# Twelve feed-forward tiles in eight products in place of seven, with the input sums four tiles later

## The chip, the cores and the metric

The kernel runs on one core of a Trainium2 chip. A core has a matrix engine (TensorE, PE in the profile, with its weight loads shown apart as PEld), three engines for elementwise work (VectorE or DVE, ScalarE or ACT, GpSimd or POOL), and a queue that issues transfers from the chip's memory (SyncE, SP). They run beside one another and wait for each other by semaphores. The metric is the device time of one execution in microseconds (us). The kernel before was timed in three runs with a median of 2261.39 us.

## What is computed

The reference is the trunk of an encoder on one sequence of 512 tokens with 1024 features, in float32. It has two layers of the form feed-forward, token mixer, feed-forward, so there are six sublayers, which the kernel numbers 0 to 5. Sublayers 0, 2, 3 and 5 are feed-forward, sublayer 1 is a state-space mixer and sublayer 4 is differential attention. Each sublayer takes its input scaled and shifted by vectors that a projection of the condition `c` gives, adds its result, gated, to the residual stream and normalizes:

```python
def swiglu(u, w_gate, w_up, w_down):
    return (jax.nn.silu(u @ w_gate) * (u @ w_up)) @ w_down
...
        mods = (cond @ ada_w[i] + ada_b[i]).reshape(b, N_SUB, 3, D_MODEL)
        gate = lambda s: (1 + mods[:, s, 2])[:, None, :]
        y = swiglu(modulate(x, mods[:, 0]), ffn_w_gate[i, 0], ffn_w_up[i, 0], ffn_w_down[i, 0])
        x = layer_norm(ALPHA * x + 0.5 * gate(0) * y, ln_g[i, 0], ln_b[i, 0])
...
        y = swiglu(modulate(x, mods[:, 2]), ffn_w_gate[i, 1], ffn_w_up[i, 1], ffn_w_down[i, 1])
        x = layer_norm(ALPHA * x + 0.5 * gate(2) * y, ln_g[i, 2], ln_b[i, 2])
```

The hidden size of the feed-forward sublayers is 2816, which is 22 tiles of 128 features.

## The kernel before

**Layout.** Features lie on the 128 partitions and the 512 tokens along the free dimension. An input `u` is eight tiles of 128 x 512. Each float32 operand is split into a rounded high part and a low part (`uh` and `ul`, `wh` and `wl`), and a product of two of them is three matmuls: high by high, high by low, low by high (`mm3`, L162). A split of a weight tile of 128 x 1024 is a copy on ACT (L119) and a subtraction on DVE (L120).

**A feed-forward layer** (`ffn`) goes through its 22 tiles in three parts of 8, 7 and 7 (`FPARTS`). In each part it makes the hidden tiles from the gate and up weights; then eight down products (`down_units`), one for each tile of the output, sum over the part's hidden tiles and are added to the residual stream by DVE (L366, `add_res`). In the last part the down products also feed the normalization, which ends the layer and makes the next layer's `uh` and `ul` (L348 to L350). When that is done, POOL scales the residual stream (L359, L360, `residual`), while the next layer's first tiles are under way.

**A hidden tile can be made in two ways.**

- Direct: two products over eight input tiles, one for gate and one for up. That is 48 matmuls of 512 columns (in tiles 0 to 2 of layers 2, 3 and 5 they are 96 of 256 columns, since the halves of the tokens are taken one after the other). SiLU on ACT (L533), a multiplication on DVE (L535) and a split of the result follow.
- In seven products (`seven`): gate and up together are regarded as a product of two-by-two blocks, which takes seven block products in place of eight, each over four pairs of input tiles. That is 84 matmuls of 256 columns. The block products need sums of the weights, made for each tile (`weight_forms`: four sums in place, L459; four splits, L449 on ACT and L450 on DVE), and sums of the inputs, made once for each layer (`input_forms`: for each of four pairs of input tiles two additions, four sums of halves and two splits, L426 to L432). DVE and ACT put the products together (L482 to L498).

**Where each is used.** The parameter `first7` of `ffn` is the first tile that is made in seven products; in layer 0 it is 22, so there all tiles are direct. The input sums are made one pair at a time at the four tiles ahead of `first7`, right after each tile's hidden result is split. In layer 0 these are tiles 18 to 21. There the sums are made as well, though nothing uses them.

**The stream.** The 72 modulation vectors of each of the two layers of the reference are made by DVE from weight tiles of 512 KB, one unit each (`ada_unit`, L180). A generator hands them out: `advance(stream, per[0])` draws `per[0]` units after each direct tile, and `advance(stream, per[1])` draws `per[1]` after each down product of the first two parts. Layers 2 and 3 draw one after a direct tile and two after a down product. A tile in seven products draws none.

**Order and buffers.** Loads go through SP's queue in program order into four buffers of 128 x 1024 (`raw`), which the stream shares. The engines' instructions are laid out by a scheduler at build time, so work of neighbouring tiles is interleaved on each engine; at run time each engine takes its list in that order. Split weights go into rings of three buffers in each of two pools (`ring`). Hidden tiles and input sums share 32 buffers (`big`).

The lines that matter for the change are these: `ffn` decides by `if f >= first7` which way a tile is made, and makes the input sums under `if first7 - 4 <= f < first7`; the calls stand at the end of `hybrid_trunk`.

Of the kernel before, what the change touches and what calls it, by code (L numbers as in the profile page):

```python
# [46 lines left out]
def hybrid_trunk(tc, xT, cb, par, cst, adaw, wgu, wdn0, wdn1, wdn2, wdt, win, wso, wqk, wv, wao, dist_in, dtp, lam_in, out):  # L47
# [17 lines left out]
    def tmp(name="tmp"):  # L65
        return tp.tile([P, T], F32, tag="t", name=name)

    def acc(tag="acc"):
        return ps.tile([P, T], F32, tag=tag, name=tag, bufs=BANKS[tag])
# [21 lines left out]
    def load(src, n=1024):  # L91
        raw = wp.tile([P, 1024], F32, tag="raw", name="raw", bufs=4)
        nc.sync.dma_start(raw[:, :n], src)
        return raw[:, :n]
# [7 lines left out]
    def split(raw, where=None):  # L102

        n = raw.shape[-1]
        if where == "a":
            hi, lo = [], []
            for o in range(0, n, T):
                r = raw[:, o : o + T]
                h, l = big(F32R, "wah"), big(F32R, "wal")
                x = nc.scalar.activation(h, r, AF.Copy)  # L110
                eng = nc.vector if first_split[0] or o else nc.gpsimd
                y = eng.tensor_tensor(out=l, in0=r, in1=h.bitcast(F32), op=ALU.subtract)  # L112
                for a, b in zip((x, y), behind):
                    tc.add_manual_dep(a.ins, b.ins.name, NOSYNC, reason="inputs before weights")
                hi.append(h)
                lo.append(l)
            return [(hi[c // T][:, c % T : c % T + P], lo[c // T][:, c % T : c % T + P]) for c in range(0, n, P)]
        hi, lo = ring()
        nc.scalar.activation(hi[:, :n], raw, AF.Copy)  # L119
        nc.vector.tensor_tensor(out=lo[:, :n], in0=raw, in1=hi[:, :n].bitcast(F32), op=ALU.subtract)  # L120
        return Unit(hi, lo, n)
# [20 lines left out]
    def split_act(src, scale=None):  # L142
        hi, lo = big(F32R, "hi"), big(F32R, "lo")
        split_into(hi, lo, src, scale)
        return hi, lo
# [22 lines left out]
    def proj(o, w, u, m=P, cols=FULL, prev=None):  # L168
        for a, b in cols:
            prev = mm3(  # L170
                o[:m, a:b], [(w[k][0], w[k][1], u[k][0][:, a:b], u[k][1][:, a:b]) for k in range(len(u))], prev
            )
        return prev
# [47 lines left out]
    def ada_stream(l, js):  # L221
        for j in js:
            ada_unit(l, j)
            if (j + 1) % 8 == 0:
                s, ty = divmod(j // 8, 3)
                n = l * 3 + s
                if ty == 1 and n > 0:
                    make_shift_scale(n)
                elif ty == 2:
                    make_gate(n)  # L230
            yield

    def advance(g, n):
        for _ in range(n):
            if g is None or next(g, "end") == "end":
                return
# [136 lines left out]
    def first_units(n):  # L373

        if n == 1:
            src = [win[e] for e in range(2)]
        elif n == 4:
            src = [wqk[0, e] for e in range(2)]
        else:
            src = [wgu[{2: 1, 3: 2, 5: 3}[n], j // 2, j % 2] for j in range(3)]  # L380
        return [split(load(x), "a") for x in src]
# [39 lines left out]
    def input_forms(u):  # L421

        for k in range(4):
            top, bot = tmp("ft"), tmp("fb")
            for o, d in ((top, k), (bot, k + 4)):
                nc.vector.tensor_tensor(out=o, in0=u[d][0].bitcast(F32), in1=u[d][1].bitcast(F32), op=ALU.add)  # L426
            t5, t7, t4, t2 = top[:, :H], top[:, H:], bot[:, :H], bot[:, H:]
            nc.vector.tensor_tensor(out=t5, in0=t5, in1=t7, op=ALU.subtract)
            nc.vector.tensor_tensor(out=t7, in0=t7, in1=t2, op=ALU.subtract)
            nc.vector.tensor_tensor(out=t2, in0=t2, in1=t5, op=ALU.add)  # L430
            nc.vector.tensor_tensor(out=t4, in0=t4, in1=t2, op=ALU.subtract)
            (th, tl), (bh, bl) = split_act(top), split_act(bot)  # L432

            def half(x, j):
                return tuple(y[:, j * H : (j + 1) * H] for y in x)

            yield {
                1: half(u[k], 0), 2: half(u[k + 4], 0), 3: half(u[k + 4], 1),
                5: half((th, tl), 0), 7: half((th, tl), 1), 4: half((bh, bl), 0), 6: half((bh, bl), 1),
            }  # L440
# [30 lines left out]
    def seven(raw_g, raw_u, forms, hs):  # L471

        w = weight_forms(raw_g, raw_u)

        def product(j, o, **kw):
            return mm3(o, [(*w[j][k], *forms[k][j]) for k in range(4)], **kw)

        A, B, C = acc(), acc(), acc("mid")
        px, sg, up = tmp("px"), tmp("sg"), tmp("up")
        y, x = px[:, :H], px[:, H:]  # L480
        product(1, A[:, :H])
        nc.scalar.activation(y, A[:, :H], AF.Copy)  # L482
        product(6, B[:, :H])
        nc.vector.tensor_tensor(out=x, in0=y, in1=B[:, :H], op=ALU.subtract)
        yield
        product(5, C[:, :H])
        last = product(2, A[:, :H], start=False)
        nc.scalar.activation(sg[:, :H], A[:, :H], AF.Silu)
        product(7, B[:, :H], start=False)
        nc.vector.tensor_tensor(out=y, in0=B[:, :H], in1=y, op=ALU.subtract)  # L490
        nc.vector.tensor_tensor(out=up[:, H:], in0=y, in1=C[:, :H], op=ALU.subtract)  # L491
        product(4, A[:, H:], after=last)
        nc.vector.tensor_tensor(out=up[:, :H], in0=y, in1=A[:, H:], op=ALU.add)
        yield
        product(3, C[:, :H], start=False)
        nc.vector.tensor_tensor(out=x, in0=x, in1=C[:, :H], op=ALU.add)
        nc.scalar.activation(sg[:, H:], x, AF.Silu)
        nc.vector.tensor_tensor(out=sg, in0=sg, in1=up, op=ALU.mult)  # L498
        hs.append(split_act(sg))


    def ffn(n, stream=None, per=(0, 0), pre=None, first7=FT):


        forms, making = [], None
        sc = ExitStack()
        extra[0] = sc.enter_context(tc.tile_pool(name=f"wx{n}", bufs=3))
        idx = {0: 0, 2: 1, 3: 2, 5: 3}[n]
        u = next_u[0]
        f = 0  # L510
        pre = pre or first_units(n)
        for pi, nf in enumerate(FPARTS):
            hs = []
            open7 = None
            for _ in range(nf):
                if f >= first7:
                    g = seven(load(wgu[idx, f, 0]), load(wgu[idx, f, 1]), forms, hs)
                    next(g)
                    if open7 is not None:
                        next(open7, None)  # L520
                    next(g)
                    open7 = g
                    f += 1
                    continue
                wg, wu = (pre.pop(0) if pre else split(load(wgu[idx, f, e])) for e in range(2))
                cols = HALVES if f < 3 and n > 0 else FULL
                tag = "mid" if f == 2 else "ln" if f == 3 and n == 0 else "acc"
                pg = acc(tag)
                proj(pg, wg, u, cols=cols)
                pu = acc(tag)  # L530
                proj(pu, wu, u, cols=cols)
                sg = tmp("sg")
                nc.scalar.activation(sg, pg, AF.Silu)  # L533
                h = tmp("h")
                nc.vector.tensor_tensor(out=h, in0=sg, in1=pu, op=ALU.mult)  # L535
                hs.append(split_act(h))
                if first7 - 4 <= f < first7:
                    making = making or input_forms(u)
                    forms.append(next(making))
                f += 1  # L540
                if f > 3 or n > 0:
                    advance(stream, per[0])

            if open7 is not None:
                next(open7, None)

            def mk(d):
                return lambda: [(d, split(load(wdn[pi][idx, d], nf * P)))]

            for _ in down_units(n, hs, [mk(d) for d in range(KT)], pi == len(FPARTS) - 1):  # L550
                if pi < 2:
                    advance(stream, per[1])
        extra[0] = None
        sc.close()
# [497 lines left out]
    advance(st0, 100)  # L1052
    ssm(1)
    st1 = ada_stream(1, range(72))
    ffn(2, st1, (1, 2), first7=4)
    ffn(3, st1, (1, 2), first7=4)
    advance(st1, 100)
    attention(4)
    ffn(5, first7=4)
    ctx.close()  # L1060


# [99 lines left out]
```

## Time and profile before

| | |
|---|---|
| median of three runs | 2261.39 us (2259.89 to 2261.66) |
| the profiled execution | 2260.94 us |
| its span, first to last instruction | 2259.2 us |
| granted TensorE clock, mean | 0.988 |
| PE busy | 2170.5 us, 96% |
| DVE busy | 1746.3 us, 77% |
| ACT busy | 989.0 us, 44% |
| POOL busy | 403.5 us, 18% |
| read from memory | 289.53 MB |

A page of the profile gives the busy time of each engine, a chain of work followed back from the last instruction, and groups of instructions by line. In a row such as `L162 PE MATMUL acc<-hi,wh 128*128 128x512 f32`, L162 is the line of the kernel, `acc` is what is written, `hi` and `wh` are what is read. A number in square brackets at the end of a row of the timeline is the time for which the engine stood idle before that instruction, with the instruction that released it. Matmuls are pipelined and their ends are modelled: the time from one to the next is what they cost. A view of stretches gives for each the busy time and count of instructions of each engine, the granted clock of TensorE (PEclk, 1.00 is full speed), the share of the transfer engines' time and the rate in GB/s. All times are counted from the start of the span.

The feed-forward layers 2, 3 and 5 begin their first product at 834.6, 1216.4 and 1880.1 us.

### The profile page before, as it was taken

The numbers are of one execution on the slowest core, as the hardware profiler recorded it, in microseconds if no ns is written. First come the engines' busy times: TensorE is split into PE (matmuls) and PEld (weight loads), VectorE is DVE, ScalarE is ACT, GpSimd is POOL, SyncE is SP. The second block draws the span as 40 slices with busy tenths as digits, with TensorE's granted clock in tenths as the row PEclk, the third lists the DMA queues.
The fourth block names the chain that finished last, engine by engine and source line by source line (L and its number), as shares of the span: only waits on it lengthen the run. The fifth ranks groups of instructions, "written<-read, shape, count | busy, mean of one in ns | idle before, by whom it ended". The sixth has DMA issues, their size and how long they took to land.

```text
span 2259.2 us, 33641 instructions
## 1 busy us (share of the span) xinstructions
PE 2170.5 (96%) x13030; PEld 1866.5 (83%) x13030; DVE 1746.3 (77%) x2850; ACT 989.0 (44%) x1648; POOL 403.5 (18%) x412
## 2 busy tenths in 40 slices
PE   7999999999999988999999899999999999899998
PEld 5788889866777677898999889899877779889897
DVE  6864668656766689998888998897866679959696
ACT  4422234567656534343453334343555544425353
POOL 3000003344222335000014200003300025100003
PEclk9999999999999999999999999999999999999999
DMA  8864652564544413646442273633211111323231
GB/s 301 281 212 161 206 169 78 124 174 141 163 125 128 126 47 112 215 140 201 145 131 76 83 252 102 234 110 115 67 57 57 57 60 63 102 86 106 91 114 46
DMA packets 88545, 296.97 MB, mean 131 GB/s; under 512 B 9536, under 2 KB 12992, under 8 KB 88384
## 3 DMA queue, kind: packets, MB, share of 16 engines
q1 hardware_dynamic: 88384, 294.81, 40.9%
q8 instruction: 102, 1.67, 0.3%
q14 instruction: 59, 0.48, 0.1%
HBM read 289.53 MB, written 5.24 MB: 130 GB/s over the span
## 4 chain that ended last, share of the span: by engine, by line
PE 54%; DVE 17%; issue 5%; ACT 3%; DMA 2%; POOL 2%; POOLq 0%; ACTq 0%; DVEq 0%; SPq 0%
PE acc L162 42%; PE mid L162 5%; DVE wl L120 2%; DVE raw L459 2%; PE mid L782 2%; DVE lo L150 1%; DVE wl L450 1%; DMA raw<-in_wdn 1%; DVE ul L350 1%; DVE raw L180 1%; PE mid L931 1%; PE ln L162 1%; DVE lt L348 1%; ACT wh L119 1%; PE ln L249 1%
## 5 line engine op out<-in xcount | busy, mean ns | idle before, releaser
L162 PE MATMUL acc<-hi,wh 128*128 128x512 f32 (+1 forms) x1488 | 506.6, 341 | 20.0 <-ACT wh L449 10.0
L162 PE MATMUL acc<-hi,wl 128*128 128x512 f32 (+1 forms) x1488 | 505.9, 340 | 5.5 <-DVE wl L450 5.5
L162 PE MATMUL acc<-lo,wh 128*128 128x512 f32 (+1 forms) x1488 | 504.9, 340 | 0.0
L162 PE MATMUL acc<-uh,wh 128*128 128x512 f32 (+1 forms) x1256 | 442.6, 353 | 4.5 <-ACT px L482 4.4
L162 PE MATMUL acc<-ul,wh 128*128 128x512 f32 (+1 forms) x1256 | 439.7, 350 | 0.1
L162 PE MATMUL acc<-uh,wl 128*128 128x512 f32 (+1 forms) x1256 | 438.5, 350 | 1.3 <-DVE wl L120 1.3
L119 ACT ACTIVATE wh<-raw 128x1024 fp32r<-128x1024 f32 (+1 forms) x234 | 239.2, 1027 | 410.1 <-PE acc L162 212.1
L120 DVE TENSOR_TENSOR wl<-raw,wh 128x1024 fp32r<-128x1024 f32 (+1 forms) x234 | 288.0, 1232 | 86.5 <-ACT wh L119 77.5
L162 PEld LDWEIGHTS acc<-hi,wh 128*128 128x128 f32 x1488 | 283.5, 191 | 58.0 <-ACT wh L449 10.6
L162 PEld LDWEIGHTS acc<-hi,wl 128*128 128x128 f32 x1488 | 284.0, 191 | 37.0 <-DVE wl L450 6.3
L162 PEld LDWEIGHTS acc<-lo,wh 128*128 128x128 f32 x1488 | 283.8, 191 | 31.2 <-DVE lo L150 1.3
L162 PEld LDWEIGHTS acc<-uh,wh 128*128 128x128 f32 x1256 | 238.3, 190 | 45.1 <-issue 9.4
L162 PEld LDWEIGHTS acc<-uh,wl 128*128 128x128 f32 x1256 | 238.2, 190 | 35.9 <-issue 3.9
L162 PEld LDWEIGHTS acc<-ul,wh 128*128 128x128 f32 x1256 | 238.5, 190 | 33.8 <-issue 4.7
L449 ACT ACTIVATE wh<-raw 128x1024 fp32r<-128x1024 f32 x162 | 170.8, 1059 | 211.1 <-DVE raw L459 107.6
L180 DVE SCALAR_TENSOR_TENSOR raw<-raw,cond 128x1024 f32<-128x1024 f32 x144 | 179.5, 1254 | 52.4 <-DMA raw<-in_adaw 52.0
L450 DVE TENSOR_TENSOR wl<-raw,wh 128x1024 fp32r<-128x1024 f32 x162 | 197.0, 1220 | 28.6 <-ACT wh L449 27.7
L112 POOL TENSOR_TENSOR wal<-raw,wah 128x512 fp32r<-128x512 f32 x13 | 19.7, 1517 | 895.8 <-ACT wah L110 308.4
L366 DVE SCALAR_TENSOR_TENSOR resid<-acc,gv,resid 128x512 f32<-128x512 f32 (+1 forms) x172 | 113.0, 659 | 76.7 <-PE acc L162 76.2
L459 DVE TENSOR_TENSOR raw<-raw 128x512 f32<-128x512 f32 x216 | 150.3, 698 | 4.4
L162 PE MATMUL mid<-uh,wh 128*128 128x256 f32 (+2 forms) x332 | 94.8, 286 | 1.0 <-DVE up L491 0.9
L162 PE MATMUL mid<-uh,wl 128*128 128x256 f32 (+2 forms) x332 | 94.0, 284 | 0.6 <-DVE wl L120 0.6
(270 smaller groups left out, 3920.1 us busy)
## 6 DMA issues: line engine op xcount, KB each, us to landing
raw<-in_wgu SPq DMA_DIRECT2D x176, 512.0 KB, 3.9
raw<-in_adaw SPq DMA_DIRECT2D x144, 512.0 KB, 4.4
raw<-in_wdn SPq DMA_DIRECT2D x64, 448.0 KB, 3.5
raw<-in_win SPq DMA_DIRECT2D x40, 512.0 KB, 3.6
raw<-in_wdn SPq DMA_DIRECT2D x32, 512.0 KB, 4.6
rw<-scr SPq DMA_DIRECT2D x32, 512.0 KB, 5.6
ch<-scr SPq DMA_DIRECT2D x32, 256.0 KB, 3.6
raw<-in_wso SPq DMA_DIRECT2D x16, 512.0 KB, 3.4
```

Of the source, the lines that this page charges most:

```text
L119: nc.scalar.activation(hi[:, :n], raw, AF.Copy)
L120: nc.vector.tensor_tensor(out=lo[:, :n], in0=raw, in1=hi[:, :n].bitcast(F32), op=ALU.subtract)
L150: y = nc.vector.tensor_tensor(out=lo, in0=src, in1=hi.bitcast(F32), op=ALU.subtract)
L162: last = nc.tensor.matmul(o, lhsT=a, rhs=b, start=start and j == 0, stop=j == n - 1, skip_group_check=not start)
L180: nc.vector.scalar_tensor_tensor(out=raw, in0=raw, scalar=1.0, in1=cond, op0=ALU.mult, op1=ALU.mult, accum_out=mods[l][:, j : j + 1],)
L249: nc.tensor.matmul(o[:, j * P : (j + 1) * P], lhsT=cols[:, j : j + 1].broadcast_to([P, P]), rhs=ident, start=True, stop=True)
L348: nc.vector.scalar_tensor_tensor(out=t, in0=res[d][:, a:b], scalar=G, in1=rb, op0=ALU.mult, op1=ALU.mult)
L366: nc.vector.scalar_tensor_tensor(out=res[d][:, a:b], in0=pd[:, a:b], scalar=gvec[n][:, d : d + 1], in1=res[d][:, a:b], op0=ALU.mult, op1=A ...
L449: nc.scalar.activation(x[0], r, AF.Copy)
L450: nc.vector.tensor_tensor(out=x[1], in0=r, in1=x[0].bitcast(F32), op=ALU.subtract)
L459: nc.vector.tensor_tensor(out=o, in0=x, in1=y, op=ALU.add)
L782: nc.tensor.matmul(py[hh * 64 : (hh + 1) * 64, cc], lhsT=lhs, rhs=rhs, start=k == 0, stop=k == 2)
```

## The change

Three calls are changed, and nothing else:

```diff
     st1 = ada_stream(1, range(72))
-    ffn(2, st1, (1, 2), first7=4)
-    ffn(3, st1, (1, 2), first7=4)
+    ffn(2, st1, (1, 2), first7=8)
+    ffn(3, st1, (1, 2), first7=8)
     advance(st1, 100)
     attention(4)
-    ffn(5, first7=4)
+    ffn(5, first7=8)
     ctx.close()
```

What `ffn` does with it, for each of the three layers:

```python
            for _ in range(nf):
                if f >= first7:
                    g = seven(load(wgu[idx, f, 0]), load(wgu[idx, f, 1]), forms, hs)
...
                if first7 - 4 <= f < first7:
                    making = making or input_forms(u)
                    forms.append(next(making))
                f += 1
                if f > 3 or n > 0:
                    advance(stream, per[0])
```

Tiles 4 to 7 are made directly, from 48 matmuls of 512 columns in place of 84 of 256. The whole first part of a layer is then direct, and the second and third parts, 14 tiles, are in seven products as before. The input sums are made at tiles 4 to 7 in place of 0 to 3. Since a direct tile draws a unit of the stream, layer 2 draws 40 units in place of 36, and layer 3 draws the remaining 32: eight at its direct tiles, 16 at the down products of its first part and eight at the first four down products of its second part.

## The prediction

> **What bounds the kernel now.** I read the page first, then the busy time in stretches, then the idle times of TensorE (PE) in the stretches that looked wrong, and last what VectorE (DVE), ScalarE (ACT) and GpSimd (POOL) did there.
>
> ```profile
> span 2259.2 us, 33641 instructions
> ...
> PE 2170.5 (96%) x13030; PEld 1866.5 (83%) x13030; DVE 1746.3 (77%) x2850; ACT 989.0 (44%) x1648; POOL 403.5 (18%) x412
> ...
> PE 54%; DVE 17%; issue 5%; ACT 3%; DMA 2%; POOL 2%; POOLq 0%; ACTq 0%; DVEq 0%; SPq 0%
> ```
>
> PE is busy 96% of the span, and the chain that ended last runs through PE for 54% and through DVE for 17%. So a change is worth what it does to PE's time, plus what it does where DVE keeps PE waiting. The next view gives busy times by stretch. The first row is feed-forward layer 2, tiles 0 to 3, from PE's first product to its last. The other three run from that last product to the residual addition of the eighth down product of the first part, that is over tiles 4 to 7 and eight down products, in layers 2, 3 and 5.
>
> ```profile
> core 0: us, PE busy (x) PEld busy (x) DVE busy (x) ACT busy (x) POOL busy (x), PEclk, DMA share, GB/s
> 834.55:886.94 52.39, 50.43 (x362) 46.94 (x362) 52.39 (x87) 21.14 (x36) 34.75 (x18) 1.00 0.32 101
> 886.94:983.43 96.49, 88.25 (x534) 78.67 (x534) 88.65 (x140) 37.53 (x51) 0.00 (x0) 0.96 0.55 186
> 1265.73:1361.15 95.42, 88.18 (x519) 78.29 (x520) 85.53 (x132) 35.05 (x49) 0.00 (x0) 0.95 0.55 184
> 1930.95:2023.84 92.89, 86.65 (x520) 76.79 (x520) 67.55 (x99) 34.83 (x49) 0.00 (x0) 0.96 0.31 103
> ```
>
> Two things are to be seen. In tiles 0 to 3 of layer 2 DVE is busy every microsecond. In the three later stretches PE is idle (96.49 - 88.25 = 8.24, 7.24 and 6.24 us), and its clock is granted at 0.96, 0.95 and 0.96. The longest of PE's idle times stand where tile 3 ends and tile 4, the first tile in seven products, begins:
>
> ```profile
> 893.47 0.58 PE L162 MATMUL acc<-hi,wh 128*128 128x256 f32 x1 [6.53 <-ACT wh L449]
> ...
> 1267.33 0.38 PE L162 MATMUL acc<-hi,wh 128*128 128x256 f32 x1 [1.60 <-ACT wh L449]
> 1270.12 0.39 PE L162 MATMUL acc<-hi,wl 128*128 128x256 f32 x1 [2.29 <-DVE wl L450]
> 1276.17 0.58 PE L162 MATMUL acc<-uh,wh 128*128 128x256 f32 x1 [2.87 <-ACT px L482]
> ...
> 1932.79 0.39 PE L162 MATMUL acc<-hi,wh 128*128 128x256 f32 x1 [1.84 <-ACT wh L449]
> 1935.58 0.58 PE L162 MATMUL acc<-hi,wl 128*128 128x256 f32 x1 [2.22 <-DVE wl L450]
> ```
>
> PE waits for tile 4's weight forms (L449, L450). They are late because DVE is:
>
> ```profile
> 859.58 3.68 POOL L359 TENSOR_TENSOR resid<-resid,rs 128x512 f32<-128x512 f32 x2
> ...
> 859.80 2.31 DVE L120 TENSOR_TENSOR wl<-raw,wh 128x1024 fp32r<-128x1024 f32 x1
> ...
> 887.09 0.41 DVE L429 TENSOR_TENSOR ft<-ft,fb 128x256 f32<-128x256 f32 x1
> ...
> 891.04 0.68 DVE L150 TENSOR_TENSOR lo<-fb,hi 128x512 fp32r<-128x512 f32 x1
> 891.64 0.68 DVE L459 TENSOR_TENSOR raw<-raw 128x512 f32<-128x512 f32 x1
> 892.36 1.06 ACT L449 ACTIVATE wh<-raw 128x1024 fp32r<-128x1024 f32 x1 [1.21 <-DVE raw L459]
> 893.98 1.22 DVE L450 TENSOR_TENSOR wl<-raw,wh 128x1024 fp32r<-128x1024 f32 x1
> ```
>
> The weight sum at 891.64 ends when ACT's L449 may start, and before it stand input sums (L429) and their splits (L150) of tiles 2 and 3. Besides, while POOL scales the residual (L359, L360; 34.75 us of POOL in the first stretch), a split over 1024 columns takes DVE 2.31 us, against 1.22 us for one of the same form at 893.98. So the input sums are made just where DVE is slowest, with the weight sums of tile 4 right behind them.
>
> **What the stall costs.** Prices of PE's work come from stretches in which it ran without a pause:
>
> ```profile
> 107.54:113.15 5.61, 5.61 (x26) 4.56 (x25) 2.52 (x4) 1.64 (x3) 0.00 (x0) 1.00 0.48 170
> 162.77:229.05 66.28, 66.28 (x290) 54.18 (x289) 32.62 (x43) 18.59 (x25) 0.00 (x0) 1.00 0.52 171
> 322.78:344.87 22.09, 22.09 (x97) 18.06 (x96) 14.81 (x25) 8.38 (x13) 0.00 (x0) 1.00 0.30 89
> 2058.91:2088.91 30.00, 30.00 (x254) 30.00 (x254) 26.95 (x41) 14.85 (x23) 0.00 (x0) 1.00 0.39 127
> ```
>
> The columns are those above. The second holds six direct tiles of layer 0: 11.05 us each, 48 matmuls of 512 columns at 0.230 us. The last holds three tiles in seven products: 10.00 us each, 84 matmuls of 256 columns at 0.119 us. (The counts hold some that straddle an end.) The stretch of layer 2 above has 192 matmuls of 512 columns (eight down products of 24) and 342 of 256: 44.2 + 40.7 = 84.9 us of work in 96.49, so 11.6 us are lost. In layer 3 it is 44.2 + 38.9 = 83.1 in 95.42, 12.3 us lost; in layer 5 83.2 in 92.89, 9.7 us. **Lost in all: 33.6 us.** The idle times, 21.7 us, and the missing clock, 0.04 x 96.49 + 0.05 x 95.42 + 0.04 x 92.89 = 12.3 us, give 34.0, so nothing else is in it.
>
> **The change part by part.**
>
> *Twelve tiles become direct* (4 to 7 of three layers). On PE each costs 11.05 in place of 10.00 us, so **+12.6 us**; PE is the bound there, and nothing covers it. [...]
>
> *DVE and ACT lose the weight forms* of these tiles: four sums, the products' combinations and two of the four splits. A direct tile with input sums beside it is in the trace: the third row, tiles 20 and 21 of layer 0, where the input sums are made as well, at 11.05 us a tile and with DVE at 14.81 of 22.09 us. That is the arrangement that tiles 4 to 7 are given.
>
> *The input sums move* from tiles 0 to 3 to tiles 4 to 7. POOL's scaling is over by then (no POOL in the stretch from 886.94), so they run at full speed. DVE has 7.4 us of work a tile by the third row; a unit of the modulation stream adds 1.25 us (below) in layers 2 and 3. That is 8.7 of 11.05 us, and PE hides it. Were that cover gone, four tiles of sums at the excess of 2.31 over 1.22 us would bring back a stall of the kind above.
>
> *Tiles 0 to 3 are relieved.* Two waits of PE in them are for weight splits behind input sums:
>
> ```profile
> 862.16 0.39 PE L162 MATMUL mid<-uh,wl 128*128 128x256 f32 x1 [0.56 <-DVE wl L120]
> 874.64 0.50 PE L162 MATMUL acc<-uh,wl 128*128 128x512 f32 x1 [0.54 <-DVE wl L120]
> ```
>
> I take both as gone, **-1.1 us**. Bounds: nothing, and 2.0 us (52.39 - 50.43, all idle time there).
>
> *The stream moves.* A direct tile draws one modulation unit, a tile in seven none, so tiles 4 to 7 draw four more in layers 2 and 3, and the last eight are missing in the second part's down products of layer 3.
>
> ```profile
> L180 DVE SCALAR_TENSOR_TENSOR raw<-raw,cond 128x1024 f32<-128x1024 f32 x144 | 179.5, 1254 | 52.4 <-DMA raw<-in_adaw 52.0
> ```
>
> Each is a load on SP's queue and 1254 ns of DVE. DVE can sit behind a late load (52.0 us over the whole run), and weight splits are queued behind it. For that I take nothing, since a PE at work covers it; the bounds are 2.9 us on either side (eight waits of 52.0/144 = 0.36 us).
>
> *Tile 8 becomes the first in seven.* Its weight forms are made beside the eight down products, as now:
>
> ```profile
> 983.43:997.28 13.85, 13.85 (x117) 13.71 (x116) 10.83 (x18) 5.29 (x9) 0.00 (x0) 1.00 0.26 79
> 1361.15:1376.77 15.62, 15.62 (x132) 15.49 (x131) 11.03 (x17) 6.09 (x9) 0.00 (x0) 1.00 0.18 63
> 2023.84:2039.39 15.55, 15.55 (x132) 15.41 (x131) 11.02 (x16) 6.09 (x9) 0.00 (x0) 1.00 0.15 41
> ```
>
> From the last residual addition to the end of tile 8, PE has no idle time in any layer. Nothing there depends on whether tile 7 was direct, so I take the 33.6 us as wholly gained. The step from a direct tile 7 to the down products costs 0.1 us a layer by the row at 107.54 (24 matmuls, 5.52, in 5.61 us).
>
> **The sum.** The profiled execution took 2260.94 us (span 2259.2), 0.45 under the median of 2261.39. 2260.94 - 33.6 - 1.1 + 12.6 + 0.3 = 2239.1; **2239 us**, 2234 to 2244 with these bounds and one dip of the clock more or less (3.4 us, see the rivals). A measurement of this kernel can tell some 0.2%, 4.5 us, from no change.
>
> **The rivals.**
>
> 1. *DVE stays behind.* For it: DVE is busy 52.39 of 52.39 us in tiles 0 to 3 of layer 2, and I remove only the sums from that. If a third of the loss remains, as shorter waits in tiles 4 to 7, the time is 2239 + 11.2 = 2250; with half of it, 2256. Against it: the third price row. 17%.
>
> 2. *The clock's dips stay.* In layer 5 no wait of PE was over 2.22 us, and the clock fell all the same. [...] If all three dips stay, 12.3 us of the gain are missing: 2251. Against it: each dip lies in the stretch with the waits, and the stretches beside them have 1.00. 6%.
>
> 3. *The stall moves to tile 8: slower.* The first tile in seven products has no predecessor whose products fill PE. If its weight forms are late after the down products, as tile 4's are now, idle time and low clock come back there, and 12.6 us stand unpaid: 2260.9 + 12.6 - 1.1 = 2272. It decides once these forms end over some 2 us after the last down product. Against it: the three rows at tile 8. 8%.
>
> 4. *Gain beyond it.* The clock also falls at the end of a layer, where the normalization stops PE:
>
> ```profile
> 1195.00:1215.00 20.00, 16.31 (x108) 15.98 (x108) 14.23 (x34) 5.97 (x12) 6.99 (x8) 0.83 0.17 58
> ```
>
> There 0.17 x 20 = 3.4 us are missing. If two such dips go with another timing: 2232. 6%.
>
> 5. *Even.* Half the loss stays and a dip is added: 2258. 3%.
>
> **How the numbers follow.** The forecast has 60%, the rivals 17, 6, 8, 6 and 3. Faster by over 0.2%: 60 + 17 + 6 + 6 = 89%; within: 3%; slower: 8%. The range takes in all of the forecast's and most of rivals 1, 2 and 4: 2231 to 2251 us.
>
> **What would show it.** Right: in layers 2, 3 and 5, tiles 4 to 7 end 11.05 us apart; no idle time of PE over 1 us and a clock of 1.00 from tile 3 to tile 8; L429 with no POOL beside it. Wrong: L449 or L450 named before the first product of tile 8 (rival 3); waits for L120 in tiles 4 to 7 (rival 1); a clock under 1.00 with PE never idle (rival 2). A direct tile longer than 11.05 us beside the stream would make the term of 12.6 us wrong.

## The result and the profile after

The changed kernel took 2234.6 us (median of four runs, 2231.13 to 2236.35), the kernel before 2260.64 us beside it (2255.46 to 2261.66). The ratio is 0.9887, with a 95% interval from 0.9868 to 0.9907: about 26 us faster. The forecast was 2239 us, in a range from 2231 to 2251.

The profiled execution of the changed kernel took 2234.43 us. From its page come the span, the busy times and the chain that ended last:

```profile
span 2232.6 us, 32613 instructions
...
PE 2168.2 (97%) x12598; PEld 1847.3 (83%) x12598; DVE 1660.7 (74%) x2718; ACT 964.5 (43%) x1600; POOL 402.0 (18%) x412
...
PE 57%; DVE 12%; issue 5%; DMA 3%; ACT 3%; POOL 2%; POOLq 0%; ACTq 0%; DVEq 0%; SPq 0%
```

PE issues 432 matmuls fewer (13030 before) but is as long busy (2170.5 us before), since those it issues are wider. DVE has 86 us less to do, and its share of the chain falls from 17 to 12%. The next view is busy times by stretch, from the first product of layers 2, 3 and 5 to the residual addition of the eighth down product of the first part, first before and then after:

```profile
834.55:983.43 148.88, 138.68 (x896) 125.60 (x896) 141.04 (x226) 58.67 (x87) 34.75 (x18) 0.98 0.47 156
...
1216.43:1361.15 144.72, 137.33 (x883) 124.94 (x882) 134.56 (x212) 53.39 (x81) 28.44 (x18) 0.96 0.43 143
...
1880.13:2023.84 143.71, 136.37 (x881) 123.61 (x882) 118.37 (x179) 54.91 (x84) 31.76 (x18) 0.98 0.27 89
```

```profile
834.01:972.36 138.35, 137.23 (x737) 117.99 (x738) 117.58 (x193) 50.40 (x71) 36.15 (x18) 1.00 0.58 187
972.36:1204.68 232.32, 225.46 (x1611) 211.72 (x1610) 203.03 (x312) 96.94 (x147) 23.46 (x18) 0.99 0.44 141
1204.68:1341.00 136.32, 136.18 (x739) 117.75 (x738) 110.22 (x176) 45.47 (x65) 27.51 (x18) 1.00 0.53 170
...
1859.79:1997.66 137.87, 136.80 (x737) 117.97 (x738) 89.88 (x135) 46.81 (x68) 27.74 (x18) 1.00 0.28 92
```

The three stretches went from 437.31 to 412.54 us, **24.8 of the 26.5 us** between the two profiled executions. PE's idle time in them fell from 24.9 us (148.88 - 138.68 and so on) to 2.3 us, and its clock is 1.00 in all three. Each of the later and earlier stretches differs by less than 0.7 us.

### The profile page after: what moved, and what is told of

Read it like the earlier page. It is cut to its first block, busy times and chain, and to the rows that moved or that the text cites. A ratio compares the mean times of both kernels' runs of the same rounds, so it can differ in the third digit from the quotient of the medians.

```text
span 2232.6 us, 32613 instructions
## 1 busy us (share of the span) xinstructions
PE 2168.2 (97%) x12598; PEld 1847.3 (83%) x12598; DVE 1660.7 (74%) x2718; ACT 964.5 (43%) x1600; POOL 402.0 (18%) x412
## 4 chain that ended last, share of the span: by engine, by line
PE 57%; DVE 12%; issue 5%; DMA 3%; ACT 3%; POOL 2%; POOLq 0%; ACTq 0%; DVEq 0%; SPq 0%
PE acc L162 46%; PE mid L162 5%; DVE wl L120 2%; PE mid L782 1%; DMA raw<-in_adaw 1%; DVE raw L180 1%; DVE ul L350 1%; PE mid L931 1%; PE ln L162 1%; DVE raw L459 1%; DMA raw<-in_wdn 1%; DVE lt L348 1%; ACT wh L119 1%; PE ln L249 1%; DVE wl L450 1%
## 5 line engine op out<-in xcount | busy, mean ns | idle before, releaser
L162 PE MATMUL acc<-uh,wh 128*128 128x512 f32 (+1 forms) x1352 | 489.5, 362 | 0.0
L162 PE MATMUL acc<-ul,wh 128*128 128x512 f32 (+1 forms) x1352 | 487.4, 360 | 0.3 <-DVE ul L1039 0.3
L162 PE MATMUL acc<-hi,wh 128*128 128x512 f32 (+1 forms) x1392 | 478.1, 344 | 9.5 <-DVE resid L366 6.6
L162 PE MATMUL acc<-uh,wl 128*128 128x512 f32 (+1 forms) x1352 | 485.9, 360 | 0.9 <-DVE wl L120 0.9
L162 PE MATMUL acc<-hi,wl 128*128 128x512 f32 (+1 forms) x1392 | 477.7, 343 | 0.0
L162 PE MATMUL acc<-lo,wh 128*128 128x512 f32 (+1 forms) x1392 | 477.2, 343 | 0.3 <-DVE lo L150 0.3
L119 ACT ACTIVATE wh<-raw 128x1024 fp32r<-128x1024 f32 (+1 forms) x258 | 264.4, 1029 | 425.6 <-PE acc L162 237.8
L120 DVE TENSOR_TENSOR wl<-raw,wh 128x1024 fp32r<-128x1024 f32 (+1 forms) x258 | 321.4, 1247 | 96.3 <-ACT wh L119 87.7
L162 PEld LDWEIGHTS acc<-hi,wh 128*128 128x128 f32 x1392 | 265.1, 190 | 45.5 <-DVE resid L366 6.5
L162 PEld LDWEIGHTS acc<-uh,wh 128*128 128x128 f32 x1352 | 255.0, 189 | 47.2 <-issue 9.0
L162 PEld LDWEIGHTS acc<-lo,wh 128*128 128x128 f32 x1392 | 265.0, 190 | 31.5 <-DVE lo L150 1.5
L162 PEld LDWEIGHTS acc<-uh,wl 128*128 128x128 f32 x1352 | 255.2, 189 | 43.1 <-issue 3.9
L162 PEld LDWEIGHTS acc<-hi,wl 128*128 128x128 f32 x1392 | 265.2, 190 | 30.7 <-issue 1.2
L162 PEld LDWEIGHTS acc<-ul,wh 128*128 128x128 f32 x1352 | 255.5, 189 | 42.1 <-issue 4.7
L449 ACT ACTIVATE wh<-raw 128x1024 fp32r<-128x1024 f32 x126 | 133.5, 1060 | 206.9 <-PE acc L162 124.7
L450 DVE TENSOR_TENSOR wl<-raw,wh 128x1024 fp32r<-128x1024 f32 x126 | 153.5, 1220 | 27.1 <-ACT wh L449 25.6
L459 DVE TENSOR_TENSOR raw<-raw 128x512 f32<-128x512 f32 x168 | 115.2, 690 | 4.1
L162 PE MATMUL mid<-uh,wh 128*128 128x256 f32 (+2 forms) x284 | 81.0, 286 | 0.8 <-DVE up L491 0.8
L162 PE MATMUL mid<-ul,wh 128*128 128x256 f32 (+2 forms) x284 | 80.3, 283 | 0.2 <-DVE ul L350 0.2
```

The lines of the kernel that those rows point to most:

```text
L162: last = nc.tensor.matmul(o, lhsT=a, rhs=b, start=start and j == 0, stop=j == n - 1, skip_group_check=not start)
L449: nc.scalar.activation(x[0], r, AF.Copy)
L450: nc.vector.tensor_tensor(out=x[1], in0=r, in1=x[0].bitcast(F32), op=ALU.subtract)
L459: nc.vector.tensor_tensor(out=o, in0=x, in1=y, op=ALU.add)
```

## The experiments

Each run is compared with the kernel before on the same chip. "Layer 2, 3, 5" are the three feed-forward layers of the change.

| run | median, us | ratio to before, 95% interval |
|---|---|---|
| the changed kernel | 2234.6 | 0.9887 [0.9868, 0.9907] |
| e1, input sums back at tiles 0 to 3 | 2254.0 | 0.9986 [0.9973, 0.9999] |
| e2, before, without input sums | 2228.5 | 0.9871 [0.9856, 0.9885] |
| e3, before, without GpSimd's scaling | 2224.9 | 0.9853 [0.9838, 0.9867] |
| e4, seven products from tile 6 on | 2238.1 | 0.9916 [0.9900, 0.9932] |
| e5, e1 with the stream held back | 2240.9 | 0.9913 [0.9894, 0.9931] |
| e6, no stream at tiles 4 to 7 | 2231.7 | 0.9873 [0.9856, 0.9890] |
| e7, seven products from tile 15 on | 2252.7 | 0.9964 [0.9949, 0.9979] |
| e8, changed kernel with the stream held back | 2242.5 | 0.9918 [0.9897, 0.9940] |
| e9, before, half of the scaling on ScalarE | 2270.4 | 1.0055 [1.0038, 1.0072] |
| e10, before, scaling on VectorE and ScalarE | 2231.5 | 0.9876 [0.9862, 0.9891] |
| e11, tile 6, four stream draws, e9's scaling | 2253.2 | 0.9970 [0.9956, 0.9983] |
| e12, four stream draws, tile 6 in layer 5 | 2231.1 | 0.9879 [0.9865, 0.9894] |

**What made the stall before: e2 and e3.** Both keep seven products from tile 4 on, and each takes one suspected cause away by leaving a part of the computation out: e2 the input sums, e3 GpSimd's scaling of the residual ahead of the three layers. So neither is a kernel to use; they only price a cause.

```diff
 # e2, in layers 2, 3 and 5
+                    if n > 0:
+                        k = f - first7 + 4
+                        forms.append({j: tuple(y[:, :H] for y in u[k + (4 if j in (2, 3) else 0)]) for j in range(1, 8)})
+                        f += 1
+                        advance(stream, per[0])
+                        continue
                     making = making or input_forms(u)
                     forms.append(next(making))
 # e3, in residual()
-            if n < 5:
+            if n in (0, 3):
```

> The kernel before (seven products from tile 4 on) with the input sums of layers 2, 3 and 5 left out: the products read slices of the input itself, which leaves out 4.4 us of VectorE for each of four tiles a layer. Theory A (the sums are the backlog): nearly all of the 33.6 us lost comes back: 2226 to 2232 us. Theory C (the change from direct tiles to tiles in seven products stalls by itself, by the chain of weight sums and splits): the waits before tile 4 stay: 2248 us or more.

> The kernel before with GpSimd's scaling of the residual stream left out ahead of layers 2, 3 and 5, so that VectorE's instructions there take their usual time. Worked out from the groups of VectorE in tiles 0 to 3 of layer 2, that is about 11 us of VectorE a layer, more than the 6 to 8 us of idle TensorE. If VectorE's slowness beside GpSimd is needed for the stall: 2226 to 2234 us. If the stall comes from the amount of work alone: 2252 us or more.

Both came out on the side of the first reading, e2 within its numbers at 2228.5 us and e3 a little below them at 2224.9 us. In the groups of VectorE by line, over tiles 0 to 3 of layer 2, the slowness beside GpSimd can be read; first the kernel before, then e3 (busy us, mean ns of one):

```profile
L120 DVE TENSOR_TENSOR wl<-raw,wh 128x1024 fp32r<-128x1024 f32 x5 | 8.7, 1734 | 0.0
...
L180 DVE SCALAR_TENSOR_TENSOR raw<-raw,cond 128x1024 f32<-128x1024 f32 x4 | 6.4, 1594 | 0.0
```

```profile
L120 DVE TENSOR_TENSOR wl<-raw,wh 128x1024 fp32r<-128x1024 f32 x5 | 6.1, 1215 | 0.0
L180 DVE SCALAR_TENSOR_TENSOR raw<-raw,cond 128x1024 f32<-128x1024 f32 x4 | 4.9, 1213 | 0.0
L450 DVE TENSOR_TENSOR wl<-raw,wh 128x1024 fp32r<-128x1024 f32 x4 | 4.9, 1213 | 0.0
```

Without the scaling, a split takes 1.2 in place of 1.7 us on average, and four weight splits for tiles in seven products (L450; a tile has three of this size) are done in a stretch in which before there was one. So the stall takes both: the sums in front of the weight forms, and VectorE's slowness beside GpSimd's scaling (1734 against 1215 ns for a split). Either one taken away is enough: over the three layers e2 gains 29 and e3 33 us, out of the 33.6 that the prediction counted as lost.

**The same without leaving anything out: e10 and e9.** In e10 the residual is scaled by VectorE and ScalarE; in e9 the multiplication stays on GpSimd.

```diff
 # e9 and e10, in residual()
-                    nc.gpsimd.tensor_scalar(
-                        out=res[d], in0=res[d], scalar1=lnag[n][:, d : d + 1],
-                        scalar2=lnab[n][:, d : d + 1], op0=ALU.mult, op1=ALU.add,
-                    )
+                    nc.scalar.activation(res[d], res[d], AF.Identity, bias=lnab[n][:, d : d + 1], scale=lnag[n][:, d : d + 1])
 # e10 alone
-                    nc.gpsimd.tensor_tensor(out=res[d], in0=res[d], in1=self.rs, op=ALU.mult)
+                    nc.vector.tensor_tensor(out=res[d], in0=res[d], in1=self.rs, op=ALU.mult)
```

> The kernel before, with the second half of the residual's scaling (L360) on ScalarE in place of GpSimd, so that GpSimd works about half as long beside tiles 0 to 3. All of the computation is kept. If VectorE's slowness beside GpSimd is what turns the backlog into a stall, half to three quarters of the 33 us of the run without scaling: 2233 to 2244 us. If each instruction of GpSimd holds VectorE up only by chance: 2250 us or more.

> The kernel before, with the first half of the scaling (L359) on VectorE and the second (L360) on ScalarE: nothing of it on GpSimd. VectorE gets eight instructions of 0.7 us a layer more, 5.6 us, and loses its slowness, some 11 us. If the slowness is the cause: 2228 to 2238 us. If the amount of VectorE's work is: 2262 us or more.

e10 took 2231.5 us: VectorE has more to do, and yet the kernel with seven products from tile 4 on is as fast as the changed one. Its weight splits (L120) are back at 1215 ns on average over tiles 0 to 3 of layer 2, as in e3. It isn't free of stalls, though. The eight instructions that VectorE took over stand together in its list (4.90 us), and in layer 2 PE waits 4.83 us for a weight split (L120) that comes behind them, with a clock of 0.87 from 858 to 885 us:

```profile
859.80 0.58 PE L162 MATMUL acc<-uh,wl 128*128 128x256 f32 x1 [4.83 <-DVE wl L120]
```

Spreading them out wasn't tried.

e9 missed, at 2270.4 us, slower than before. Its timeline shows ScalarE first and PE second:

```profile
862.71 0.81 ACT L360 ACTIVATE resid<-resid,lnab,lnag 128x512 f32<-128x512 f32 x1 [1.42 <-POOL resid L359]
863.93 0.81 ACT L360 ACTIVATE resid<-resid,lnab,lnag 128x512 f32<-128x512 f32 x1 [0.41 <-POOL resid L359]
...
868.99 1.05 ACT L119 ACTIVATE wh<-raw 128x1024 fp32r<-128x1024 f32 x1
```

```profile
870.09 0.58 PE L162 MATMUL mid<-uh,wh 128*128 128x256 f32 x1 [7.41 <-ACT wh L119]
```

ScalarE's list now has eight instructions that wait for GpSimd one after the other, and the weight copy (L119) that PE needs stands behind them. The expectation had counted GpSimd's time and not who would queue behind it.

**The place of the sums alone: e1 and e5.** e1 is the changed kernel with the sums at tiles 0 to 3.

```diff
 # e1; first7 is 8 in layers 2, 3 and 5, FT in layer 0
-                if first7 - 4 <= f < first7:
+                if (0 if first7 < FT else first7 - 4) <= f < (4 if first7 < FT else first7):
```

> Tiles 4 to 7 direct as in the changed kernel, the input sums back at tiles 0 to 3. Theory A (the stall is the weight forms of the first tile in seven products standing behind the input sums on VectorE): no weight forms follow the sums now, so only waits of 1 to 3 us a layer can return in tiles 0 to 3: 2236 to 2242 us. Theory B (making the sums beside GpSimd's scaling is by itself what costs): at least half of the 26 us gained is lost: 2248 us or more.

2254.0 us (2249.9 to 2258.74 in ten runs): nearly the whole gain is lost, as theory B had it, but not in the way that it says. In the view by stretch, with the same ends as above, layer 5 of e1 takes just what it took in the changed kernel, while layer 2 takes 148.34 us in place of 138.35 and layer 3 takes 145.78 in place of 136.32:

```profile
835.05:983.39 148.34, 139.41 (x737) 118.93 (x738) 122.78 (x193) 49.96 (x71) 35.28 (x18) 0.98 0.53 174
1215.11:1360.89 145.78, 139.33 (x739) 119.44 (x738) 115.47 (x176) 44.78 (x65) 30.69 (x18) 0.98 0.49 159
1878.89:2016.76 137.87, 136.77 (x737) 117.94 (x738) 95.07 (x136) 46.73 (x68) 31.35 (x18) 1.00 0.29 92
```

The two layers lose 10.0 and 9.5 us, which is all of the 19.5 us between the two profiled executions (2253.88 and 2234.43). Layer 5 has no stream. In layer 2 PE waits once for long, ahead of the down products, and the timelines of PE and of VectorE show for what:

```profile
941.65 0.80 PE L162 MATMUL acc<-hi,wh 128*128 128x512 f32 x1 [6.68 <-ACT hi L149]
```

```profile
937.57 1.22 DVE L180 SCALAR_TENSOR_TENSOR raw<-raw,cond 128x1024 f32<-128x1024 f32 x1 [2.16 <-DMA raw<-in_adaw]
...
939.10 1.23 DVE L180 SCALAR_TENSOR_TENSOR raw<-raw,cond 128x1024 f32<-128x1024 f32 x1 [0.30 <-DMA raw<-in_adaw]
...
940.25 0.68 DVE L535 TENSOR_TENSOR h<-sg,acc 128x512 f32<-128x512 f32 x1
```

The build-time scheduler has put units of the stream ahead of tile 7's multiplication in VectorE's list. They wait for their loads, the multiplication waits behind them, and PE, with its 6.68 us, waits for both. In layer 3 it is the same, with 6.03 us. In tiles 0 to 3, where the sums stand beside GpSimd's scaling, PE waits for VectorE's splits only twice, 1.1 us in all and in layer 2, as before the change. Theory D, made from this, was tried in e5, which orders the first part's units behind the last multiplication:

```diff
 # e5, in ada_unit; hold[0] is the part's last hidden multiplication while part 0's down products are laid out
+        if hold[0] is not None:
+            tc.add_manual_dep(x.ins, hold[0].ins.name, NOSYNC, reason="hidden tiles before the stream")
```

> Direct tiles 4 to 7 with the input sums at tiles 0 to 3, as in the run before, and the stream's units of the first part's down products ordered behind the part's last hidden multiplication on VectorE. Theory D (what cost 20 us there was that VectorE's list has those units ahead of tile 7's multiplication, and each waits for its load): the waits of 6.7 and 6.0 us ahead of the down products and the low clock behind them go, 2234 to 2239 us. If the sums' place under GpSimd's scaling costs by itself: 2248 us or more.

2240.9 us: about two thirds of the loss come back (13 of 20 us by the medians, 16 of 22 by the ratios, each of which is taken on one chip), and the wait ahead of the down products is gone from layers 2 and 3. It stayed 2 us above the expectation; the units held back meet tile 8's weight forms, and PE waits there, in layer 2 as shown and in layer 3 for 0.54 and 1.28 us, with a clock of 0.83 over 10 us in both places (974 to 984 and 1347 to 1357 us):

```profile
975.77 0.39 PE L163 MATMUL acc<-hi,wh 128*128 128x256 f32 x1 [0.95 <-ACT wh L452]
977.56 0.38 PE L163 MATMUL acc<-hi,wl 128*128 128x256 f32 x1 [1.28 <-DVE wl L453]
```

(The lines are further down there: L163 is L162 of the kernel before, and L452 and L453 are its L449 and L450.)

**The stream in the changed kernel: e6 and e8.** e6 draws no unit at tiles 4 to 7; e8 holds the stream back as e5 does, in both parts.

```diff
 # e6
-                if f > 3 or n > 0:
+                if n == 0 and f > 3 or n > 0 and f < 5:
```

> The changed kernel, but tiles 4 to 7 draw no unit of the stream (layers 2 and 3 have 36 units each again). If the move of the stream is hidden, as predicted: 2233 to 2237 us. If the units drawn at tiles 4 to 7 are what keeps later units from being put ahead of tile 7's multiplication (theory D in the changed kernel), the wait ahead of the down products comes back: 2243 us or more.

> The changed kernel with the stream's units of the first and second parts' down products ordered behind the part's last hidden multiplication. TensorE waits 2.4 us at the end of the second part in each of layers 2 and 3 for VectorE, with stream units ahead in its list. Theory D: these waits shrink, 2228 to 2233 us. If they are the seven products' own chain: 2234 to 2237 us.

e6 took 2231.7 us, a little below its first expectation; its interval overlaps that of the changed kernel, so that the draws cost or save anything isn't shown. No stall ahead of the down products came back. e8 was meant to be faster and was slower, 2242.5 us: the units held back make tile 8's and tile 15's weight forms late, with waits of PE up to 2.16 us. Units that run early in idle moments of VectorE are of use here, and holding all of them back costs 7.9 us by the medians, more than the waits that it removes.

**Where seven products begin: e4 and e7.** Only `first7` differs.

> Seven products from the seventh tile on, input sums at tiles 2 to 5. Half of the changed tiles go back to 10.0 us from 11.05: 6.3 us less than the changed kernel if no stall comes back: 2228 us. Theory A expects some of it back, since the weight forms of tile 6 stand right behind the sums again, but after GpSimd is done: 2229 to 2240 us. If the stall belongs to any first tile in seven products inside a part (theory C): 2250 us or more.

> Seven products from the sixteenth tile on, so 21 more tiles are direct, input sums at tiles 11 to 14. Theory A with the price of 1.05 us a tile: plus 22 us, less some 4 us of waits at the end of the second part in layers 2 and 3: 2250 to 2258 us. If the gain came from relieving VectorE in general: 2238 us or less.

e7 is 18.1 us above the changed kernel, for 21 more direct tiles. At 1.05 us each that would be 22. The part that is missing is of the size of PE's waits at the end of the second part in layers 2 and 3, 2.4 us each in the changed kernel, which are gone; but new waits of 1.70 and 0.57 us stand ahead of the first down products of its layer 2, so the sum doesn't close to better than some 2 us. The price itself is in the trace: in e7's layer 5, VectorE's multiplications (L535) of tiles 8 to 14 stand 11.05 us apart (once 10.97). So the price of a direct tile holds far from tile 4 as well, and relieving VectorE in general isn't what pays. e4 gives 2238.1 us: the half price of 6.3 us is eaten by waits behind tile 5 in layers 2 and 3, such as these in its layer 2:

```profile
910.86 0.39 PE L162 MATMUL acc<-uh,wh 128*128 128x256 f32 x1 [1.11 <-ACT px L482]
914.20 0.39 PE L162 MATMUL mid<-hi,wh 128*128 128x256 f32 x1 [1.54 <-ACT hi L149]
```

**Looking for a faster one: e11 and e12.** e11 has seven products from tile 6 on in the three layers, e6's four draws and e9's scaling; e12 is e6 with `first7=6` in layer 5.

> Looking for a faster one: seven products from the seventh tile on, a unit of the stream at the first four tiles only, the second half of the scaling on ScalarE. The price of direct tiles is 6.3 us less than in the changed kernel; the waits of 3.3 us behind tile 5 in layers 2 and 3 should shrink with a faster VectorE: 2226 to 2232 us. If they come from the weight forms alone: 2234 us or more.

> The changed kernel with a unit of the stream at the first four tiles only, and seven products from the seventh tile on in the last layer, where no stream runs and where that layer took 1.0 us less in the run with six direct tiles: 2229 to 2233 us. If nothing of this is more than noise: 2234 to 2237 us.

e11 missed: 2253.2 us, with e9's wait of PE for L119 back in layer 2 (7.39 us). e12 took 2231.1 us. The changed kernel, e6, e10 and e12 have intervals that overlap, so no version that keeps the whole computation is shown to beat the changed one. e10's scaling combined with e6's stream wasn't tried.

## Why the prediction was right, step by step

- **The lost 33.6 us.** Right. PE's idle time in the three layers is gone but for what stands in tiles 0 to 3 (the starts of layers 2 and 5), and the clock is 1.00. e2 and e3 show that the cause was read rightly, and add what the profile couldn't tell: the two causes don't add up, and either alone is nearly harmless (in the first parts of the three layers, e2 leaves no wait of PE over 1 us, and e3 none over 0.3 us beyond the first two tiles). One label is off: the stretches that the prediction takes for tiles 4 to 7 begin after tile 4's first block product, 12 matmuls that need no weight sum (885.36 to 886.65 us in layer 2), so PE's long wait is inside tile 4 and not ahead of it, and in layer 2 the stretch ends 18 matmuls into tile 8. The counts of 342, 327 and 328 matmuls carry both, so the loss stands.
- **+12.6 us for direct tiles.** Right. In PE's timeline of the changed kernel's layer 2, the first product of tile 4 and the first down product are 44.18 us apart, four tiles of 11.05:

```profile
883.17 0.39 PE L162 MATMUL acc<-uh,wh 128*128 128x512 f32 x1
...
927.35 0.39 PE L162 MATMUL acc<-hi,wh 128*128 128x512 f32 x1
```

In layers 3 and 5 it is 44.19 us. In layer 5, tiles 6 and 7 end 11.04 us apart with PE busy throughout (the two ends in VectorE's timeline):

```profile
1942.36 0.69 DVE L535 TENSOR_TENSOR h<-sg,acc 128x512 f32<-128x512 f32 x1 [2.47 <-PE acc L162]
1953.40 0.69 DVE L535 TENSOR_TENSOR h<-sg,acc 128x512 f32<-128x512 f32 x1 [2.47 <-PE acc L162]
```

- **-1.1 us in tiles 0 to 3.** Right: the two waits for L120 are gone from layer 2; in e1, with the sums back, they return as 0.57 and 0.53 us.
- **The stream at nothing.** Right in the sum, but the bound of 2.9 us was too narrow. It was worked out from the mean wait of a unit. What a late unit costs is what stands behind it in VectorE's list, and e1 shows 6.68 us of PE at one place, and a clock of 0.83 from 930 to 950 us around it, for units that the scheduler had put ahead of tile 7. The changed kernel has units there as well: in layer 2 three run between the multiplications of tiles 6 and 7, where e1 has four, but none of the three waits for its load, and in e1 three of the four do. Nothing in the prediction told that it would come out so; that the term held is in part luck. Why the list and the loads fall so in e1 and not in the changed kernel stays open. That the sums at tiles 4 to 7 fill the list isn't enough as an answer: e7 has no sums there either, and PE's wait at that place is 1.70 us in its layer 2 and none in layer 3.
- **The missing 4.7 us.** The profiled execution is 2234.43 against the 2239.1 of the sum. The three stretches give 24.8 in place of 21.8 us (33.6 + 1.1 - 12.6 - 0.3). Of these 3.0 us, 1.8 are only displaced: in the first stretch before, 18 matmuls of tile 8 were already done, and three are after. The stretch behind it in layer 2 does these 15 matmuls more and is 0.7 us shorter still (233.00 before), with 2.0 us less idle time of PE; that gain was not forecast, and what made it wasn't tested. The stretch ahead of layer 2, that of attention and the last one are 0.5, 0.2 and 0.4 us shorter. The medians of the kernel before moved by 2.8 us between the groups of runs (2257.87 to 2260.64), so a difference of this size doesn't need a cause of its own.
- **Rival 1** (VectorE stays behind) fell: tiles 4 to 7 take PE 11.05 us each in all three layers, with no wait for L120. Already ahead of them, in the changed kernel, PE is busy throughout a stretch of tiles 0 to 3 of layer 2 in which GpSimd is busy as well (by stretch):

```profile
860.00:886.00 26.00, 26.00 (x164) 23.50 (x164) 20.06 (x21) 10.61 (x12) 25.18 (x13) 1.00 0.82 263
```

- **Rival 2** (the dips stay) fell: they went with the waits, and the clock is 1.00 in the three stretches. That waits of at most 2.22 us were too short for layer 5's dip was the author's estimate, and no run shows it; in e8 the clock fell behind waits of 0.40 and 1.39 us.
- **Rival 3** (the stall moves to tile 8) didn't happen in the changed kernel, but its mechanism exists: e5 and e8 have it, with some 2 us of waits a layer and a low clock behind them (0.91 from 1340 to 1360 us in both), once the stream's units stand in front of tile 8's weight forms.
- **Rival 4** (more gain by the dips at the ends of layers) fell: at the end of layer 2 the clock is 0.83 over 20 us after (1184 to 1204 us) as before. The dip at the end of attention did go (0.96 before, 1.00 after, over the last 40 us ahead of layer 5), but PE is idle 1.3 us longer there, and the time is the same to 0.2 us.

## What to carry to other kernels

Here the form with fewer products was worth its saving of 1.05 us a tile only where the engine that prepares its operands had time left; look for that stage by stage, since the same form that lost 11.6 us at layer 2's tiles 4 to 7 was free of waits further into the layer (from 1120.80 to 1160.79 us of the kernel before, PE is busy throughout and VectorE 36.82 of the 39.99 us). The backlog at tile 4 had two causes that were both needed (2228.5 us without the one, 2224.9 without the other), so before giving up the cheaper products, try to take away the other (here, GpSimd's work beside VectorE: e10, 2231.5 us). When an instruction that waits for a load is moved in an engine's list, bound its cost by what the engine has queued behind it (6.68 us of PE in e1), and not by its mean wait (0.36 us).

## What the runs showed of the hardware that wasn't expected

The clock of TensorE fell behind waits shorter than the 2.22 us that the prediction found beside layer 5's dip. In e8 the stretch from 1340 to 1360 us has a clock of 0.91, and PE's waits in it are 0.40 and 1.39 us; it has no other of 0.1 us or more from 1290 us on. The clock is 1.00 up to 1352 us, 0.62 and 0.53 in the next two stretches of 2 us, and 1.00 again from 1356 us:

```profile
1340.00:1360.00 20.00, 18.21 (x102) 16.21 (x101) 17.07 (x26) 6.92 (x10) 0.00 (x0) 0.91 0.56 188
```

```profile
1350.73 0.38 PE L163 MATMUL mid<-hi,wh 128*128 128x256 f32 x1 [0.40 <-ACT wh L452]
1352.63 0.58 PE L163 MATMUL acc<-hi,wh 128*128 128x256 f32 x1 [1.39 <-ACT wh L452]
```

So in e8 1.8 us of waits in two pieces, 2.3 us from the start of the first to the end of the second, went with a dip. In the changed kernel, waits of PE of 0.79, 0.41 and 1.21 us at the end of layer 2's second part, within 12 us, passed at a clock of 1.00 (the stretch from 983 to 1060 us). What decides between the two isn't shown.
